# Hybrid diffusion backbone on one core: sums of squares read from the SBUF copies, values split first

## The chip, the core and the metric

The kernel runs on one core of a Trainium2 chip. A core has a matrix engine (TensorE; PE in the profile, with its weight loads as PEld), a vector engine (VectorE; DVE), an activation engine (ScalarE; ACT), GpSimd (POOL) and SyncE (SP), which issues DMA here. Each engine runs its own queue in order, and engines wait for each other by semaphores. Matrix products land in banks of PSUM; everything else lives in SBUF. The metric is the device time of one execution in microseconds, lower is better.

## What is computed

Two layers over 256 latent tokens and 256 context tokens, 512 rows of width 1024 in four row tiles `tt` of 128. In each layer a normed input goes through one wide projection into three mixers (a bidirectional Mamba-2 scan, windowed attention, multi-head latent attention) and gates; the mixers are projected back, gated and summed, and a SwiGLU network follows. What matters here is that keys, queries and latents are RMS-normed, each over its own last axis:

```
def rms_norm(x, g):
    y = xf * lax.rsqrt(jnp.mean(xf * xf, axis=-1, keepdims=True) + EPS)
    return (y * g.astype(F32)).astype(x.dtype)

def kv_heads(k, v):                       # windowed attention
    return rms_norm(k.reshape(shp), k_g), v.reshape(shp)

kv = (rms_norm(ckv, kv_lat_g) @ w_ukv).reshape(bsz, n, MLA_HEADS, MLA_NOPE + MLA_V)
k_nope = rms_norm(kv[..., :MLA_NOPE], k_g[:MLA_NOPE])      # latent attention; the rest of kv are values
q = (rms_norm(cq, q_lat_g) @ w_uq).reshape(bsz, n, MLA_HEADS, MLA_QK)
```

So each of these norms needs a sum of squares of a product that lies in PSUM, and the product itself in SBUF. Values are not normed.

## The kernel before

**Products in three parts.** Every fp32 product is made of three matmuls (`mm3`, L147 to L149): both factors are split into a high part `hi` and a rest `lo`, and hi·hi, hi·lo and lo·hi are summed in a PSUM bank. `hilo` (L150) splits a PSUM result so: ACT writes the high part (L154), then DVE subtracts it from the same bank (L155; with a scale L157 and L158). `wsplit` (L124) does the same with weights that a DMA brought: ACT at L133, DVE at L135, into three buffers (NHI), with a priority of 200 over other work. Attention's probabilities are split by `hilo` too (`pth`, `ptl`).

**Banks.** `PS` hands out PSUM tiles of one bank: four tagged `mm`, two `s`, two `t`. A product that needs a bank waits until the last reader of the result in it is done.

**The stages that the change touches.** `ssm_inproj` copies the latents `lat` and the rope keys `kro` (L725, L726) and squares both (L727, L728). `swa_kv` makes the keys and values of windowed attention: four banks, one for each row tile, 256 key columns and 256 value columns each. For each tile ACT copies the keys (`kraw`, L1063), squares both heads with a running sum into `ssk` (L1066, twice), and `hilo` splits the values into `vh` and `vl`. Behind the four tiles DVE scales `ssk` (L1070), POOL raises it to the power -1/2 (`rsk`, L161), and the keys are multiplied by it (L1076: on DVE in layer 0, on POOL in layer 1). DVE then rotates the first two tiles (`ro`, `rt`, L606 to L614), and PE transposes them (L1089). `swa_q` copies and squares the queries (L1104, L1106). `mla_prep` does so with the query latents (L1208, L1210). `mla_pair` runs four times in each layer, for two heads at a time: one bank for each tile again, with two squares (L1247), the key copy (L1248) and the split of the values, and then for the queries a square (L1266) and a copy (`qraw`, on DVE for even tiles of layer 0, else on ACT).

**What sets the order.** The stages are generators. `weave` and `braid` run them between the products of the gates (`gates`, L1354), the scan of the Mamba branch (`z`, `xs`, `ef`, `eb`, `cb`, `yo` and `hst` in the rows) and attention. A scheduling framework then lays the instructions into one fixed queue for each engine, from the order of the code, its priorities and its own estimates of durations, and puts in the semaphore waits. It keeps two engines from reading the same PSUM bank at the same time: in the queues below, a reader of a bank waits for the reader ahead of it on the other engine.

## Time and profile before

| | us |
|---|---|
| median of 3 runs (lowest, highest) | 1848.68 (1847.68, 1849.12) |
| the profiled execution | 1848.97 |
| its span in the trace | 1847.2 |
| PE busy in it | 1801.7 (98%) |
| DVE busy | 1406.7 (76%) |
| ACT busy | 920.5 (50%) |
| POOL busy | 268.2 (15%) |

The span is what the trace covers; the 1.8 us beside it lie around the program. The mean granted clock of PE was 0.997 of full speed. In a timeline row the number in brackets is how long that engine stood idle before the row, and what ended the wait; a row with no bracket began as soon as its engine was free or waited too briefly to be listed. In a row of waits the three numbers are us in total, times, and the longest one.

### The profile page before, as it was taken

Reading aid. Unit: us, or ns where it says so; the run is one execution under the profiler, and the core shown is the slowest. Engines: PE = TensorE matmul, PEld = TensorE weight load, DVE = VectorE, ACT = ScalarE, POOL = GpSimd, SP = SyncE. Lnnn points to the kernel's source line nnn. Section 1 sums busy time; section 2 is a strip of 40 time slices with the busy share of each in tenths; the row PEclk is TensorE's granted clock in tenths of the full one; section 3 lists DMA queues with packets and bytes.
Section 4 is the critical chain, followed back from the end, with each engine's and each line's share of the span. In section 5 each row is a group of like instructions: output and inputs, shape, how many; then the busy total and the mean of one; then the engine's idle time right before and its main releaser. Section 6 shows DMA issues by size and latency. Waiting matters only on the chain.

```text
span 1847.2 us, 28430 instructions
## 1 busy us (share of the span) xinstructions
PE 1801.7 (98%) x10198; PEld 1541.2 (83%) x10198; DVE 1406.7 (76%) x3094; ACT 920.5 (50%) x2026; POOL 268.2 (15%) x242
## 2 busy tenths in 40 slices
PE   8999999999999999999999999999999999999999
PEld 3886777788878888898888888886779988899999
DVE  3896876798798885569888875797788688786654
ACT  2557674455555653342323222547756767455442
POOL 1004432100013331100000000002420022210000
PEclk9999999999999999999999999999999999999999
DMA  8334352454443333535556553335334332255564
GB/s 303 92 105 148 116 175 97 153 187 154 151 152 105 99 120 119 185 115 198 188 186 201 184 189 117 104 104 182 109 132 147 107 95 88 90 180 171 183 181 139
DMA packets 101405, 270.22 MB, mean 146 GB/s; under 512 B 11504, under 2 KB 14320, under 8 KB 101264
## 3 DMA queue, kind: packets, MB, share of 16 engines
q1 hardware_dynamic: 94032, 254.37, 42.5%
q10 hardware_dynamic: 5904, 9.71, 1.5%
q0 software_dynamic: 1328, 4.33, 0.6%
q8 instruction: 80, 1.31, 0.3%
q14 instruction: 61, 0.50, 0.1%
HBM read 256.70 MB, written 11.67 MB: 145 GB/s over the span
## 4 chain that ended last, share of the span: by engine, by line
PE 70%; DVE 6%; ACT 3%; issue 3%; POOL 1%; DMA 1%; SPq 0%; POOLq 0%; DVEq 0%; ACTq 0%
PE mm L147 21%; PE mm L148 21%; PE mm L149 21%; DVE lo L135 2%; PE t L647 1%; ACT hi L133 1%; PE s L147 1%; PE s L149 1%; PE s L148 1%; DVE ptl L155 0%; DVE cv L814 0%; PE t L1317 0%; DMA eb<-scr 0%; DVE eb L962 0%; POOL xd L903 0%
## 5 line engine op out<-in xcount | busy, mean ns | idle before, releaser
L133 ACT ACTIVATE hi<-raw 128x1024 fp32r<-128x1024 f32 (+1 forms) x350 | 356.6, 1021 | 575.6 <-PE mm L148 316.4
L135 DVE TENSOR_TENSOR lo<-raw,hi 128x1024 fp32r<-128x1024 f32 (+1 forms) x350 | 426.0, 1220 | 194.7 <-ACT hi L133 192.8
L147 PE MATMUL mm<-hh,hi 128*128 128x512 f32 (+1 forms) x1280 | 438.6, 345 | 2.2 <-DVE vl L155 1.5
L149 PE MATMUL mm<-hh,lo 128*128 128x512 f32 (+1 forms) x1280 | 436.0, 341 | 0.9 <-DVE lo L135 0.9
L148 PE MATMUL mm<-hl,hi 128*128 128x512 f32 (+1 forms) x1280 | 436.1, 342 | 0.7 <-DVE hl L400 0.7
L147 PEld LDWEIGHTS mm<-hh,hi 128*128 128x128 f32 x1280 | 241.7, 190 | 30.0 <-DVE vl L155 2.0
L149 PEld LDWEIGHTS mm<-hh,lo 128*128 128x128 f32 x1280 | 242.5, 190 | 28.6 <-DVE lo L135 1.3
L148 PEld LDWEIGHTS mm<-hl,hi 128*128 128x128 f32 x1280 | 242.6, 190 | 28.4 <-DVE hl L400 1.3
L147 PE MATMUL mm<-hi,hh 128*128 128x512 f32 (+2 forms) x368 | 142.6, 388 | 3.5 <-DVE z L871 1.4
L149 PE MATMUL mm<-hi,hl 128*128 128x512 f32 (+2 forms) x368 | 137.8, 382 | 1.8 <-DVE hl L400 1.8
L148 PE MATMUL mm<-lo,hh 128*128 128x512 f32 (+2 forms) x368 | 139.5, 379 | 0.0
L271 DVE CUSTOM_DVE_ANT_0 junk<-mraw,crow,mod 128x512 bf16<-128x512 f32 x160 | 120.2, 751 | 5.2 <-DMA mraw<-in_w_modT 2.9
L271 DVE CUSTOM_DVE_ANT_0 junk<-mraw,crow 128x512 bf16<-128x512 f32 x160 | 110.2, 689 | 12.0 <-DMA mraw<-in_w_modT 10.7
L154 ACT ACTIVATE pth<-t 128x256 fp32r<-128x256 f32 x160 | 60.3, 388 | 50.8 <-DVE ptl L155 42.2
L147 PEld LDWEIGHTS mm<-hi,hh 128*128 128x128 f32 x368 | 70.0, 190 | 17.9 <-DVE z L871 2.5
L149 PEld LDWEIGHTS mm<-hi,hl 128*128 128x128 f32 x368 | 69.7, 191 | 14.0 <-DVE hl L400 2.1
L148 PEld LDWEIGHTS mm<-lo,hh 128*128 128x128 f32 x368 | 70.0, 190 | 11.9 <-issue 2.9
L147 PE MATMUL mm<-acth,hi 128*128 128x512 f32 (+1 forms) x198 | 72.7, 367 | 0.6 <-DVE xl L1416 0.6
L149 PE MATMUL mm<-acth,lo 128*128 128x512 f32 (+1 forms) x198 | 72.4, 365 | 0.0
L148 PE MATMUL mm<-actl,hi 128*128 128x512 f32 (+1 forms) x198 | 72.4, 365 | 0.0
L814 DVE SCALAR_TENSOR_TENSOR cv<-cx,c_kb,cv 128x508 f32<-128x508 f32 (+3 forms) x96 | 70.6, 736 | 1.8 <-ACT cv L805 0.4
L155 DVE TENSOR_TENSOR ptl<-t,pth 128x256 fp32r<-128x256 f32 x160 | 65.4, 415 | 7.8 <-ACT pth L154 7.4
(422 smaller groups left out, 3973.1 us busy)
## 6 DMA issues: line engine op xcount, KB each, us to landing
raw<-in_w_fi SPq DMA_DIRECT2D x88, 512.0 KB, 3.4
mraw<-in_w_modT SPq DMA_DIRECT2D x160, 256.0 KB, 4.5
raw<-in_w_g SPq DMA_DIRECT2D x48, 512.0 KB, 3.3
raw<-in_w_p SPq DMA_DIRECT2D x48, 512.0 KB, 3.3
raw<-in_w_fo SPq DMA_DIRECT2D x32, 512.0 KB, 3.9
raw<-in_w_xbc SPq DMA_DIRECT2D x24, 512.0 KB, 3.5
wm<-in_w_mod SPq DMA_DIRECT2D x32, 256.0 KB, 5.4
raw<-in_w_z SPq DMA_DIRECT2D x16, 512.0 KB, 3.3
```

The costliest lines, as they stand in the source:

```text
L133: nc.scalar.activation(hi[:, :n], raw[:, :n], AF.Copy)
L135: eng.tensor_tensor(lo[:, :n], raw[:, :n], hi[:, :n].bitcast(F32), ALU.subtract)
L147: mm(out, a[0], b[0], start=start, stop=False)
L148: mm(out, a[0], b[1], start=False, stop=False)
L149: mm(out, a[1], b[0], start=False, stop=stop)
L154: nc.scalar.activation(hi, src, AF.Copy)
L155: nc.vector.tensor_tensor(lo, src, hi.bitcast(F32), ALU.subtract)
L271: nc.vector.tensor_tensor_reduce(junk, raw[j], self.crow[2 * s + j], 0.5, o if j else 0.0, ALU.mult, ALU.add, o)
L647: nc.tensor.transpose(tp[:, i * P : (i + 1) * P], pt[:, i * P : (i + 1) * P], self.ident)
L814: nc.vector.scalar_tensor_tensor(r3(v)[:, :, o], r3(x)[:, :, i], w[:, m, j : j + 1], r3(v)[:, :, o], ALU.mult, ALU.add)
```

## The change

All sums of squares of these stages read the copy in SBUF and no longer the bank. In `swa_kv` the split of the values stands ahead of the key copy of each tile, and the squares of all four tiles stand in a second loop. In `swa_q` the squares of all tiles stand behind the copies. In `mla_pair` each tile has the split first, then the key copy, then the squares; the query copy stands ahead of its square. By count 138 squares change their source: L727 8, L728 8, L1066 16, L1106 12, L1210 6, L1247 64, L1266 24. No instruction is added or taken away. Lines of the new kernel stand 1 to 4 further down (L1063 becomes L1064, L1066 L1069, L1070 L1072, L1076 L1078, L1089 L1091, L1247 L1252, L1248 L1249).

```
@@ -724,8 +724,8 @@ ssm_inproj
             self.copy(l and tt % 2 == 0, lat[tt], ps[:, 0:256])
             nc.scalar.activation(kro[:, tt, :], ps[:, 256:320], AF.Copy)
-            nc.scalar.activation(sq[:, 0:256], ps[:, 0:256], AF.Square, accum_out=ssl[:, tt : tt + 1])
-            nc.scalar.activation(sq[:, 256:320], ps[:, 256:320], AF.Square, accum_out=ssl[:, 4 + tt : 5 + tt])
+            nc.scalar.activation(sq[:, 0:256], lat[tt], AF.Square, accum_out=ssl[:, tt : tt + 1])
+            nc.scalar.activation(sq[:, 256:320], kro[:, tt, :], AF.Square, accum_out=ssl[:, 4 + tt : 5 + tt])
@@ -1060,11 +1060,13 @@ swa_kv
         for tt in range(4):
             o = slice((tt % 2) * 256, (tt % 2) * 256 + 256)
+            self.hilo(vh[tt // 2][:, o], vl[tt // 2][:, o], pss[tt][:, 256:512])
             nc.scalar.activation(kr[tt // 2][:, o], pss[tt][:, 0:256], AF.Copy)
+        for tt in range(4):
             sq = self.U(name="sq")
             for j in range(2):
-                nc.scalar.activation(sq[:, 0:P], pss[tt][:, j * P : (j + 1) * P], AF.Square, accum_out=ss[:, tt, j : j + 1])
-            self.hilo(vh[tt // 2][:, o], vl[tt // 2][:, o], pss[tt][:, 256:512])
+                o = (tt % 2) * 256 + j * P
+                nc.scalar.activation(sq[:, 0:P], kr[tt // 2][:, o : o + P], AF.Square, accum_out=ss[:, tt, j : j + 1])
@@ -1103,7 +1105,8 @@ swa_q
             nc.scalar.activation(qr[tt], pss[tt], AF.Copy)
             sq[tt] = self.U(name="sq")
-            nc.scalar.activation(sq[tt], pss[tt], AF.Square)
+        for tt in tts:
+            nc.scalar.activation(sq[tt], qr[tt], AF.Square)
@@ -1207,7 +1210,7 @@ mla_prep
-            nc.scalar.activation(sq[:, 0:384], pss[tt][:, 0:384], AF.Square, accum_out=ss[:, tt : tt + 1])
+            nc.scalar.activation(sq[:, 0:384], cq[tt][:, 0:384], AF.Square, accum_out=ss[:, tt : tt + 1])
@@ -1242,11 +1245,11 @@ mla_pair, keys and values
+            self.hilo(o3(vh[tt // 2]), o3(vl[tt // 2]), pv[:, :, 1, :])
+            nc.scalar.activation(o3(kr[tt // 2]), pv[:, :, 0, :], AF.Copy)
             sq = self.U(name="sq")
             for j in range(2):
-                nc.scalar.activation(sq[:, 0:P], pv[:, j, 0, :], AF.Square, accum_out=ss[:, tt, j : j + 1])
-            nc.scalar.activation(o3(kr[tt // 2]), pv[:, :, 0, :], AF.Copy)
-            self.hilo(o3(vh[tt // 2]), o3(vl[tt // 2]), pv[:, :, 1, :])
+                nc.scalar.activation(sq[:, 0:P], kr[tt // 2][:, o][:, j * P : (j + 1) * P], AF.Square, accum_out=ss[:, tt, j : j + 1])
@@ -1263,8 +1266,8 @@ mla_pair, queries
-            nc.scalar.activation(sq[:, 0:384], ps[:, 0:384], AF.Square)
             self.copy(l == 0 and tt % 2 == 0, qr[tt][:, 0:384], ps[:, 0:384])
+            nc.scalar.activation(sq[:, 0:384], qr[tt][:, 0:384], AF.Square)
```

In the queues below a row is one instruction: its line, its operation, what it writes and reads, and the engines that it waits for (`Activation` is ACT, `Pool` POOL, `DMAHW...` a transfer). A row without brackets waits for nothing that its engine has not waited for already.

In ACT's queue at the window keys of layer 1, this stood before. `mm_12782` to `mm_12785` are the banks of the four row tiles, `hi_13159` a weight of the third gate product from there, `hi_13203` of the fourth:

```order
L1063 ACTIVATE kraw_13003<-mm_12782 128x256 [waits PE_49]
L1066 ACTIVATE sq_13007,ssk_13005<-mm_12782 128x128
L1066 ACTIVATE sq_13007,ssk_13005<-mm_12782 128x128 [waits Activation_49]
L154 ACTIVATE vh_12999<-mm_12782 128x256
L1063 ACTIVATE kraw_13003<-mm_12783 128x256 [waits PE_49]
```

Each tile has these four rows; `hi_13159` stands behind the third tile and `hi_13203` behind the fourth. In the same place ACT has now:

```order
L154 ACTIVATE vh_12999<-mm_12782 128x256 [waits PE_49]
L1064 ACTIVATE kraw_13003<-mm_12782 128x256 [waits DVE_49]
L154 ACTIVATE vh_12999<-mm_12783 128x256 [waits PE_49]
L1064 ACTIVATE kraw_13003<-mm_12783 128x256 [waits DVE_49]
L154 ACTIVATE vh_13000<-mm_12784 128x256 [waits PE_49]
L1064 ACTIVATE kraw_13004<-mm_12784 128x256 [waits DVE_49]
L1069 ACTIVATE sq_13018,ssk_13005<-kraw_13003 128x128 [waits Activation_49]
L133 ACTIVATE hi_13159<-raw_13157 128x1024 [waits DMAHW4_49,PE_49]
L154 ACTIVATE vh_13000<-mm_12785 128x256
...
L133 ACTIVATE hi_13203<-raw_13201 128x1024 [waits DMAHW1_49,PE_49]
L1064 ACTIVATE kraw_13004<-mm_12785 128x256 [waits DVE_49]
```

Every key copy has come behind the split's DVE half and waits for DVE; in the gap stand five squares, and two squares follow the last row, with a gate copy between them. On DVE, in the same stretch, stood before:

```order
L998 TENSOR_TENSOR z_12664<-z_12664,xs_12434 128x512 [waits Pool_49]
L155 TENSOR_TENSOR vl_13001<-mm_12782,vh_12999 128x256 [waits PE_49,Activation_49]
L155 TENSOR_TENSOR vl_13001<-mm_12783,vh_12999 128x256 [waits PE_49,Activation_49]
L155 TENSOR_TENSOR vl_13002<-mm_12784,vh_13000 128x256 [waits PE_49,Activation_49]
L135 TENSOR_TENSOR lo_13160<-raw_13157,hi_13159 128x1024 [waits DMAHW4_49,Activation_49]
L1070 TENSOR_SCALAR ssk_13005<-ssk_13005 128x8 [waits Activation_49]
```

And now:

```order
L155 TENSOR_TENSOR vl_13001<-mm_12782,vh_12999 128x256 [waits Activation_49]
L998 TENSOR_TENSOR z_12664<-z_12664,xs_12434 128x512 [waits Pool_49]
L155 TENSOR_TENSOR vl_13001<-mm_12783,vh_12999 128x256 [waits Activation_49]
L155 TENSOR_TENSOR vl_13002<-mm_12784,vh_13000 128x256 [waits Activation_49]
L135 TENSOR_TENSOR lo_13160<-raw_13157,hi_13159 128x1024 [waits DMAHW4_49,Activation_49]
L155 TENSOR_TENSOR vl_13002<-mm_12785,vh_13000 128x256 [waits PE_49,Activation_49]
L135 TENSOR_TENSOR lo_13204<-raw_13201,hi_13203 128x1024 [waits DMAHW1_49,PE_49,Activation_49]
L1072 TENSOR_SCALAR ssk_13005<-ssk_13005 128x8 [waits Activation_49]
```

The first `vl` went ahead of `z`, which waits for POOL, and the scaling of `ssk` went behind the fourth `vl` and `lo_13204`. In layer 0 ACT's queue at the window keys reads now:

```order
L154 ACTIVATE vh_1937<-mm_1692 128x256 [waits PE_49]
L154 ACTIVATE vh_1937<-mm_1693 128x256 [waits PE_49]
L1064 ACTIVATE kraw_1941<-mm_1692 128x256 [waits DVE_49]
L1064 ACTIVATE kraw_1941<-mm_1693 128x256 [waits DVE_49]
L154 ACTIVATE vh_1938<-mm_1694 128x256 [waits PE_49]
L1064 ACTIVATE kraw_1942<-mm_1694 128x256 [waits DVE_49]
L1069 ACTIVATE sq_1956,ssk_1943<-kraw_1941 128x128 [waits Activation_49]
L133 ACTIVATE hi_2130<-raw_2128 128x1024 [waits DMAHW2_49,PE_49]
...
L1064 ACTIVATE kraw_1942<-mm_1695 128x256 [waits DVE_49]
```

Before, it had the four rows of each tile in the order shown for layer 1, and the second to fourth `vl` stood on DVE behind a `z` that waits for POOL, as they do now. The scaling of `ssk` stood ahead of the fourth `vl` and stands behind it now. In the gap are the fourth split and five squares.

## Rows read from the trace of the kernel before

**Rows 1.** Page, part 1: busy us (share of the span) xinstructions.

```profile
PE 1801.7 (98%) x10198; PEld 1541.2 (83%) x10198; DVE 1406.7 (76%) x3094; ACT 920.5 (50%) x2026; POOL 268.2 (15%) x242
```

**Rows 2.** Waits of PE, whole span: us in total, times, longest us.

```profile
PE mm L147 <- ACT pth L154: 5.0, 10, 0.9
...
PE mm L147 <- DVE vl L155: 1.5, 1, 1.5
...
PE t L982 <- DVE kTl L158: 1.4, 1, 1.4
```

**Rows 3.** Groups of ACT by line and shape: count | busy us, mean ns.

```profile
L947 ACT ACTIVATE eb<-eb,du 128x128 f32<-128x128 f32 x96 | 36.4, 389 | 1.5 <-DMA eb<-scr 1.5
...
L1066 ACT ACTIVATE sq<-mm 128x128 f32<-128x128 f32 x16 | 4.4, 276 | 0.3
```

**Rows 4.** DVE timeline: start us, us, line, operation [idle before <-releaser]; latent queries.

```profile
500.43 0.56 DVE L141 COPY qraw<-mm 128x384 f32<-128x384 f32 x1 [0.95 <-ACT sq L1266]
```

**Rows 5.** DVE timeline, window keys of layer 1.

```profile
1307.33 0.69 DVE L998 TENSOR_TENSOR z<-z,xs 128x512 f32<-128x512 f32 x1 [3.99 <-POOL xs L992]
...
1307.94 1.08 DVE L155 TENSOR_TENSOR vl<-mm,vh 128x256 fp32r<-128x256 f32 x3
...
1310.07 0.16 DVE L1070 TENSOR_SCALAR ssk<-ssk 128x8 f32<-128x8 f32 x1
...
1314.82 0.51 DVE L606 TENSOR_TENSOR ro<-kraw,rs 128x256 f32<-128x256 f32 x1
...
1318.12 0.41 DVE L614 TENSOR_TENSOR ro<-ro,rt 128x256 f32<-128x256 f32 x1
```

**Rows 6.** ACT timeline, same stretch.

```profile
1303.27 0.37 ACT L1063 ACTIVATE kraw<-mm 128x256 f32<-128x256 f32 x1
...
1303.53 0.27 ACT L1066 ACTIVATE sq<-mm 128x128 f32<-128x128 f32 x1
...
1304.19 0.38 ACT L154 ACTIVATE vh<-mm 128x256 fp32r<-128x256 f32 x1
...
1306.91 1.06 ACT L133 ACTIVATE hi<-raw 128x1024 fp32r<-128x1024 f32 x1
```

**Rows 7.** POOL timeline, same stretch.

```profile
1310.31 1.65 POOL L161 TENSOR_TENSOR rsk<-ssk,mhalf 128x8 f32<-128x8 f32 x1 [3.01 <-DVE ssk L1070]
...
1312.03 3.02 POOL L1076 TENSOR_TENSOR kraw<-kraw,rsk 128x512 f32<-128x512 f32 x2
```

**Rows 8.** PE timeline, same stretch: first gate product, first key transposes.

```profile
1308.41 0.39 PE L147 MATMUL mm<-hh,hi 128*128 128x256 f32 x1 [1.53 <-DVE vl L155]
...
1319.97 0.38 PE L1089 MATMUL t<-c_ka,ro 128*128 128x128 f32 x2
```

**Rows 9.** DVE timeline, window keys of layer 0.

```profile
221.71 0.69 DVE L998 TENSOR_TENSOR z<-z,xs 128x512 f32<-128x512 f32 x1 [0.94 <-POOL xs L992]
...
225.22 0.16 DVE L1070 TENSOR_SCALAR ssk<-ssk 128x8 f32<-128x8 f32 x1
...
227.17 1.29 DVE L1076 TENSOR_TENSOR kraw<-kraw,rsk 128x512 f32<-128x512 f32 x2 [1.45 <-POOL rsk L161]
...
229.29 1.22 DVE L135 TENSOR_TENSOR lo<-raw,hi 128x1024 fp32r<-128x1024 f32 x1 [0.83 <-ACT hi L133]
...
235.90 1.23 DVE L135 TENSOR_TENSOR lo<-raw,hi 128x1024 fp32r<-128x1024 f32 x1 [1.07 <-ACT hi L133]
...
243.89 0.41 DVE L614 TENSOR_TENSOR ro<-ro,rt 128x256 f32<-128x256 f32 x1
```

**Rows 10.** PE timeline, second key transpose of layer 0.

```profile
244.36 0.33 PE L1089 MATMUL t<-c_ka,ro 128*128 128x128 f32 x1 [0.90 <-DVE ro L614]
```

**Rows 11.** Waits of PE in 540:620, 630:720 and 1530:1610 (latent pairs).

```profile
PE mm L147 <- ACT pth L154: 0.9, 1, 0.9
...
PE mm L147 <- ACT pth L154: 1.7, 4, 0.8
...
PE mm L147 <- ACT pth L154: 1.2, 2, 0.6
```

## The prediction

> **What bounds the kernel now.** I read the page first: PE is busy 98% of the span, DVE 76%, ACT 50% [rows 1]. So ACT has time to spare on average, and work given to it or taken from it moves the end only where PE stands and waits. The next view is therefore the table of PE's waits. For the banks that this change wants to empty sooner it holds a single entry, "PE mm L147 <- DVE vl L155", 1.5 us, once [rows 2]; that entry is the ceiling of what a bank handed over earlier can give directly. The largest entry is a wait for `pth`, an ACT instruction of attention, 5.0 us in ten pieces [rows 2]. Then I read timelines of ACT, DVE and POOL around the two window-key stages, since there DVE, POOL and PE depend on the last square, and last the queues of the new kernel against those of the old.
>
> **What one square costs.** The count does not change, the source does. An ACT instruction of 128x128 takes 276 ns from PSUM (L1066) and 389 ns from SBUF (L947, another function) [rows 3]. These are durations that overlap their neighbours: a 0.37 us copy at 1303.27 is followed by a square at 1303.53 in the same queue [rows 6]. So 113 ns is the upper bound for one square; zero is the lower bound; I take half, 0.05 us, since about a tenth of a us of each duration lies under the next one. For 138 squares that is 7 us (bounds 0 and 15.6) on an engine that idles half the span. I cost it at nothing except in the two chains below, where eight squares lie in a row: 0.4 us each.
>
> The Trainium skill ("Perfetto Trace Analysis", section "Optimizing Scalar/DVE Operations") speaks against this change: it gives ScalarE a fixed access overhead of about 93 ns on SBUF and about 51 ns on PSUM, so a read from the copy is the dearer one. By it a square would cost 42 ns more, an estimate of 5.8 us over 138 and 0.3 us in each chain; the rows above point the same way.
>
> **What the order costs.** The framework does not let two engines read a bank together. The trace of before shows the rule from the other side: a DVE copy of queries stands 0.95 us idle at 500.43 until ACT's square has left the bank [rows 4]. Eight such copies get free of the square, and that wait sits on DVE where PE does not wait, so I count nothing for it. The price is that each `kraw` copy, formerly ahead of the split, now waits for DVE's `vl` of its bank: 8 in `swa_kv`, 32 in `mla_pair`. Whatever DVE is stuck on, ACT is then stuck on too, and behind it in ACT's queue stand the squares, the weights' `hi` and the gates' copies.
>
> **Layer 1, window keys.** Bank 0 is full at 1303.27, when ACT's first copy starts [rows 6]. Now `vh` (0.38) and the first `vl` (0.42; it stands ahead of `z` now) and `kraw` (0.37) empty it by about 1304.5, where before `vl` came at 1307.94 behind a `z` that waited 3.99 us for POOL [rows 5]. PE's first gate product then needs no wait and starts at 1308.41 - 1.53 = 1306.88 [rows 8]. Gain: **1.5 us**.
>
> Then the second `kraw` waits for the second `vl`, which is still behind `z`: `vl` at 1307.94 to 1308.36. ACT stands from 1304.8 to 1308.4 with nothing else to do. From there, in the new order: `kraw` 0.3, `vh` 0.3, `vl` 0.4, `kraw` 0.3, one square 0.5 (it needs the copy's end, and a read of the sum) make 1310.2; the weight `hi` takes 1.06 [rows 6], `vh` 0.3, five squares at 0.38 make 1313.4; the next `hi` 1.06, `kraw`, a square, a gate's copy and the last square together 1.5 make 1315.9. Before, `ssk` was scaled at 1310.07 [rows 5]. Now it is scaled at about 1316.0, 5.9 us later. POOL's `rsk` (1.65) and the first half of its key product (1.51 of 3.02) follow [rows 7] and end at 1319.4. Before, that half ended at 1313.5 and the rotation began at 1314.82, because DVE had other work in between [rows 5]; now DVE waits for it. The rotation is thus 4.6 us late, and ends, one `eb` shorter between, some 4.3 us behind its old end of 1318.53 [rows 5], at 1322.8. PE reaches the transposes at 1319.97 - 1.53 = 1318.44 [rows 8] and stands 4.4 us. Net of the gain: +2.9. The 1.4 us that PE waits for `kTl` soon after [rows 2] shrink by some 0.4, as PE comes later by 2.9 and `kTl` by about 2.5. **+2.5 us** in all. Bounds: -1.5, if ACT does not stand behind `z` and the rotation stays inside its old slack of 1.4 us; +4.0, if all of the lateness arrives and nothing shrinks.
>
> **Layer 0, window keys.** Here the first `vl` came ahead of `z` before too, and PE had no bank wait to lose. The second `kraw` waits for the `vl` behind `z` (221.71, waiting for POOL) [rows 9], so ACT goes on at about 222.8. The same list of steps then ends with `ssk` at about 229.3 where it was at 225.22: 4.1 us late. The keys' product with `rsk` on DVE moves with it, from 227.17 to 231.3. Behind it DVE had 0.83 us of idle at 229.29 and 1.07 us at 235.90 [rows 9], both for a weight's `hi` that need not move; these take up 1.9. The last `ro` at 243.89 [rows 9] comes 2.2 us later, and PE, which already waited 0.90 for it [rows 10], waits about 3. **+2.0 us**, bounds 0 (all taken up) and +3.
>
> **Latent pairs and the rest.** In `swa_q`, `mla_prep` and `ssm_inproj` no wait of PE hangs on a bank or a square: 0, bounds ±1. In the eight pairs ACT loses two squares ahead of each split and gets a wait for DVE; where PE waits there, it is for `pth` in seven cases, 0.9 + 1.7 + 1.2 = 3.8 us [rows 11]. I take 0, with bounds -3.8 (all of these go) and +4 (half a us more for each pair, about one `vl`).
>
> **The sum.** 1848.97 (the profiled execution, 0.29 above the median) + 2.5 + 2.0 = 1853.5; against the median of 1848.68 that is 1853.2. I say **1853 us**.
>
> **The rivals.** *Not slower: the banks win.* Place: the eight pairs, and the gate product at 1308.41. Before, 0.66 us of squares (1303.53 to 1304.19 in the window keys, alike in the pairs) stood ahead of the split of every bank [rows 6]. If a `kraw` waits for its `vl` for less than that 0.66, each bank is free sooner, `pth` queued behind gets its turn sooner, and PE gains up to 3.8 + 1.5: 1848.7 - 5.3 = 1843.4, with half of it 1846. Against it speaks the 3.99 us of DVE at `z`, six times that point; for it, that most `vl` of the pairs have no such `z` ahead.
>
> *Nothing arrives.* The late squares are there, but DVE's and PE's slack takes them up, or the two terms and the gain of 1.5 cancel: 1848 to 1851. For it speaks that PE waited at neither rotation by more than 0.9 before; against it, that the lateness is three times the slack.
>
> *The pairs pay too.* ACT parked behind DVE holds `pth` and `prob` back in the pairs, where both engines are fuller than elsewhere: at half a us to a whole one for each of the eight, 4 to 8 more, 1857 to 1861.
>
> *The change doesn't do what it says.* A bank is not emptied earlier at all where `kraw` waits for `vl` and `vl` is late; that is the forecast's own mechanism, and needs no chance of its own.
>
> **How the numbers follow.** Forecast (1851.5 to 1855.5) 0.42; the banks win (1843.4 to 1848) 0.22; nothing arrives 0.22; the pairs pay 0.14. The measurement can tell about 0.2%, 3.7 us, from no change, so slower begins at 1852.4 and faster below 1845.0. Three quarters of the forecast and all of the pairs' rival are slower: 0.31 + 0.14 = 0.45. About half of the banks' rival is faster: 0.12. The rest is 0.43. The range of 8 in 10 leaves out the lower part of the banks' rival (0.13) and the upper part of the pairs' (0.07): 1846 to 1858. The forecast's own range is 1851.5 to 1855.5.
>
> **What would show it.** Right: no wait of PE at the first gate product of layer 1; an ACT idle of about 3.6 us before the second `kraw`, ended by DVE `vl`; `ssk` near 1316; PE waiting some 4 us for `ro` at the transposes of layer 1 and 3 at those of layer 0. Wrong: `ssk` before 1311 there, or PE waits for `ro` under 1 us; then the lateness was taken up, or the steps between the waits are shorter than I made them. A sum of waits for `pth` that moved by over 2 us would hand the result to the pairs.

## The result: 0.83% slower, more than three times what was forecast

The changed kernel takes 1863.79 us (median of 4 runs, 1862.49 to 1865.13) against 1848.18 us (4 runs of the kernel before beside them), a ratio of 1.0083 with a 95% interval of 1.0071 to 1.0095. The sign was right, the size was not: +15.6 us measured, +4.5 forecast, and the time lies above the stated range.

| us | before | after |
|---|---|---|
| median | 1848.18 | 1863.79 |
| span of the profiled execution | 1847.2 | 1862.2 |
| PE busy | 1801.7 | 1808.2 |
| PE idle (span less busy) | 45.5 | 54.0 |

PE issues the same 10198 matmuls. Of 15.0 us more span 8.5 are waits, and 6.5 are matmuls that took longer. Part 1 of the page of the changed kernel (busy us, share of the span, instructions), to be read beside [rows 1]:

```profile
PE 1808.2 (97%) x10198; PEld 1544.0 (83%) x10198; DVE 1409.9 (76%) x3094; ACT 925.9 (50%) x2026; POOL 265.9 (14%) x242
```


The waits of PE in the changed kernel (what waited, for whom; then us in total, times, the longest), beside [rows 2]:

```profile
PE t L1091 <- DVE ro L614: 6.6, 4, 3.2
PE t L647 <- DVE ptl L155: 5.1, 5, 2.4
PE mm L147 <- ACT pth L154: 4.7, 10, 0.8
PE t L1287 <- DVE kTl L158: 2.1, 1, 2.1
```


The wait of 1.5 us for `vl` at the first gate product is gone from the table, as the change means it. The waits for `ro` rose from 0.9 to 6.6 us, and those of the probabilities' transposes for `ptl` from 1.3 to 5.1 us. The wait for `pth`, with which two of the rivals worked, did not move (5.0 and 4.7).

### The profile page after: what moved, and what is told of

It is laid out like the page before. It is cut to its first block, busy times and chain, and to the rows that moved or that the text cites. A ratio compares the mean times of both kernels' runs of the same rounds, so it can differ in the third digit from the quotient of the medians.

```text
span 1862.2 us, 28415 instructions
## 1 busy us (share of the span) xinstructions
PE 1808.2 (97%) x10198; PEld 1544.0 (83%) x10198; DVE 1409.9 (76%) x3094; ACT 925.9 (50%) x2026; POOL 265.9 (14%) x242
## 4 chain that ended last, share of the span: by engine, by line
PE 68%; DVE 6%; issue 3%; ACT 3%; POOL 2%; DMA 2%; SPq 0%; POOLq 0%; ACTq 0%; DVEq 0%
PE mm L147 21%; PE mm L148 20%; PE mm L149 20%; DVE lo L135 2%; PE t L647 1%; ACT hi L133 1%; DMA mraw<-in_w_modT 1%; PE s L147 1%; PE s L149 1%; PE s L148 1%; DVE ptl L155 0%; POOL gate L1396 0%; DVE junk L271 0%; DVE cv L814 0%; PE t L1320 0%
## 5 line engine op out<-in xcount | busy, mean ns | idle before, releaser
L148 PEld LDWEIGHTS mm<-lo,hh 128*128 128x128 f32 x368 | 69.7, 189 | 11.9 <-issue 2.9
```

Source lines behind the costliest of these rows:

```text
L148: mm(out, a[0], b[1], start=False, stop=False)
```

## Where the time went

PE's matmuls can be paired by their number in the two traces, since there are as many in both. The difference of their start times, taken at a few places, tells in which stretch the changed kernel falls back. This is worked out from the traces' start times (in each place the median over 25 matmuls); stretches are in time of the kernel before, and the experiments of the next section stand beside. PE's own order is not the same everywhere: between 575 and 607 us it differs from the kernel before in all kernels but e6 and e10, so a bound in there sets different matmuls side by side. The rows 563-583 and 583-613 therefore count only together. Three rows set apart by "of which" or "together" have their bounds where the orders agree.

| stretch, what runs there | after | e1 | e2 | e3 | e4 | e5 | e6 | e8 | e9 | e10 | e11 | e12 |
|---|---|---|---|---|---|---|---|---|---|---|---|---|
| 242-252, window keys, layer 0 | 3.6 | 0.0 | 3.7 | 0.0 | 0.0 | 0.0 | 0.0 | 2.3 | 0.0 | 0.0 | 0.0 | 0.0 |
| 388-423, window attention, layer 0 | 2.8 | 2.0 | 2.0 | 2.8 | 1.9 | 0.0 | 1.8 | 0.0 | 0.0 | 0.0 | 0.0 | 0.0 |
| 548-563, latent pairs, layer 0 | 1.2 | 0.8 | 0.3 | 0.0 | 0.0 | 0.3 | 0.0 | 0.0 | 0.0 | 0.0 | 0.0 | 0.2 |
| 563-583, the same | 4.5 | 4.1 | 2.4 | 3.8 | 2.7 | 2.5 | 0.0 | 4.9 | 3.3 | 0.0 | 1.8 | 1.0 |
| 583-613, the same | -1.7 | -1.7 | -1.7 | -1.7 | -1.7 | -1.7 | 0.0 | -1.7 | -1.7 | 0.0 | -1.5 | -1.2 |
| 548-613, the three together | 4.0 | 3.2 | 1.0 | 2.1 | 1.0 | 1.0 | 0.0 | 3.2 | 1.6 | 0.0 | 0.3 | 0.0 |
| 613-701, the same | 2.5 | 2.6 | 2.5 | 1.2 | 1.3 | 1.3 | 0.1 | 1.6 | 0.7 | 0.0 | 0.1 | 2.1 |
| of which 671-701 | 1.4 | 1.5 | 1.3 | 0.0 | 0.1 | 0.0 | 0.0 | 1.4 | 0.1 | 0.0 | 0.1 | 1.0 |
| 1283-1331, window keys, layer 1 | 3.0 | 0.0 | 3.0 | 1.0 | 0.2 | 0.0 | 0.0 | 3.0 | 0.0 | -0.1 | 0.0 | 0.0 |
| 1486-1598, latent pairs, layer 1 | 0.0 | 1.5 | -1.5 | -0.5 | 2.1 | -0.1 | -0.2 | 0.8 | -0.1 | -1.5 | 0.0 | -0.1 |
| of which 1530-1598 | 1.1 | 1.1 | -0.1 | 1.3 | 2.3 | 0.0 | 0.0 | 2.5 | 0.0 | 0.0 | 0.0 | -0.1 |
| whole trace | 15.0 | 10.1 | 10.1 | 6.9 | 7.3 | 3.9 | 1.8 | 11.8 | 2.1 | -3.9 | -0.4 | 3.1 |

What is missing to the last row lies in small pieces and in the first 242 us; the differences there, -2.2 (e10) to +1.9 (e5), arise before 200 us, ahead of any edit of these two, and so differ from execution to execution. So the window keys cost 6.6 us, the latent pairs of layer 0 6.6, and the window attention of layer 0 2.8. The 0.0 of the pairs of layer 1 hides 1.1: in the trace of the kernel before PE ran at 0.50 of full clock in 1518 to 1521, and in that of the changed kernel it did not, which gives 1.0 back. Every trace is one execution, and a stretch at half clock that comes in one and not in another is worth 1 to 1.5 us in such a table (last section).

**Window keys of layer 1.** Three timelines of the changed kernel follow (start, duration, engine, line, operation, and in brackets the idle time ahead of it with what ended that); to compare with [rows 5 to 7], subtract 11.9 us, by which the trace is late at 1283. First ACT:

```profile
1316.02 0.39 ACT L1064 ACTIVATE kraw<-mm 128x256 f32<-128x256 f32 x1 [0.49 <-DVE vl L155]
...
1321.13 0.38 ACT L1064 ACTIVATE kraw<-mm 128x256 f32<-128x256 f32 x1 [4.45 <-DVE vl L155]
...
1322.28 0.38 ACT L1064 ACTIVATE kraw<-mm 128x256 f32<-128x256 f32 x1 [0.49 <-DVE vl L155]
...
1327.44 0.30 ACT L1069 ACTIVATE sq<-kraw 128x128 f32<-128x128 f32 x1
```


DVE in the same stretch:

```profile
1315.57 0.42 DVE L155 TENSOR_TENSOR vl<-mm,vh 128x256 fp32r<-128x256 f32 x1 [0.32 <-ACT vh L154]
1319.24 1.52 DVE L998 TENSOR_TENSOR z<-z,xs 128x512 f32<-128x512 f32 x1 [3.26 <-POOL xs L992]
1320.68 0.41 DVE L155 TENSOR_TENSOR vl<-mm,vh 128x256 fp32r<-128x256 f32 x1
...
1327.87 0.17 DVE L1072 TENSOR_SCALAR ssk<-ssk 128x8 f32<-128x8 f32 x1
...
1330.91 1.24 DVE L606 TENSOR_TENSOR ro<-kraw,rs 128x256 f32<-128x256 f32 x1 [1.86 <-POOL kraw L1078]
...
1334.10 0.41 DVE L614 TENSOR_TENSOR ro<-ro,rt 128x256 f32<-128x256 f32 x1
```


POOL in the same stretch:

```profile
1316.56 2.66 POOL L992 TENSOR_TENSOR xs<-xs,yo 128x512 f32<-128x512 f32 x2
1319.17 1.04 POOL L903 TENSOR_TENSOR xd<-xs,du 128x512 f32<-128x512 f32 x1
1328.12 1.65 POOL L161 TENSOR_TENSOR rsk<-ssk,mhalf 128x8 f32<-128x8 f32 x1 [7.90 <-DVE ssk L1072]
1329.84 2.04 POOL L1078 TENSOR_TENSOR kraw<-kraw,rsk 128x512 f32<-128x512 f32 x2
```


The first `vl` (1315.57) stands ahead of `z` now and the first copy follows it. Then the second copy waits 4.45 us for a `vl` that stands behind `z`, which itself waits for POOL and takes 1.52 us, beside POOL's `xd`, where it took 0.69. The last square runs at 1327.44 and `ssk` is scaled at 1327.87, that is 1316.0 in the old count, to the tenth what the working gave; that is luck, since the wait ended 0.8 us later than forecast (1309.2 in the old count for 1308.4) and the steps behind it took 6.6 us and not 7.5. The rotation ends at 1334.5, or 1322.6 in the old count (forecast 1322.8).

The page "PSUM — Partial Sum Buffer" of the Trainium skill (section "PSUM bank collisions raise a hardware error") says that software has to keep reads of one bank by two engines apart, reads of ScalarE and VectorE too. The trace shows the framework doing so, for other columns of the bank too: the copy starts only when `vl` has ended, 4.45 us later than ACT was free. What unguarded reads would do no run here shows.

The timeline of PE in the changed kernel, behind that:

```profile
1333.43 0.47 PE L1091 MATMUL t<-c_ka,ro 128*128 128x128 f32 x1 [3.18 <-DVE ro L614]
1334.56 0.47 PE L1091 MATMUL t<-c_ka,ro 128*128 128x128 f32 x1 [0.67 <-DVE ro L614]
```


The windows of the same stretch (from and to, their length, then busy us and count of PE, PEld, DVE, ACT and POOL, the granted clock, the DMA share, GB/s):

```profile
1329.00:1332.00 3.00, 1.24 (x11) 1.04 (x9) 1.14 (x2) 3.00 (x9) 2.80 (x3) 1.00 0.75 240
1332.00:1335.00 3.00, 0.91 (x3) 0.62 (x4) 3.00 (x16) 2.89 (x8) 0.00 (x0) 0.54 0.00 1
1335.00:1338.00 3.00, 3.00 (x16) 3.00 (x15) 3.00 (x5) 1.01 (x4) 1.37 (x1) 0.50 0.23 70
1338.00:1341.00 3.00, 3.00 (x22) 2.89 (x21) 3.00 (x8) 1.22 (x3) 0.11 (x1) 0.82 0.90 262
```


PE waits 3.18 and 0.67 us, 3.85 together (forecast 4.4). The windows show what the working did not hold: behind the wait the clock stands at 0.50, the lower of the two levels, 1.2 GHz, until past 1338, and the same 256-column matmuls start 0.21 us apart where they started 0.12 apart. That adds 2.0 us. The wait for `kTl` that followed in the kernel before is hidden by it and gives its 1.4 [rows 2] back.

**Window keys of layer 0.** The same, with 0.55 and 2.17 us of waiting where there were 0.90 [rows 10]. PE's timeline in the changed kernel:

```profile
243.30 0.30 PE L1091 MATMUL t<-c_ka,ro 128*128 128x128 f32 x1 [0.55 <-DVE ro L614]
245.76 0.33 PE L1091 MATMUL t<-c_ka,ro 128*128 128x128 f32 x1 [2.17 <-DVE ro L614]
```


Its windows, with half clock behind the second wait:

```profile
244.00:247.00 3.00, 1.24 (x7) 1.09 (x8) 3.00 (x8) 1.07 (x2) 0.42 (x1) 0.97 0.23 87
247.00:250.00 3.00, 3.00 (x9) 2.32 (x8) 2.73 (x10) 2.92 (x10) 0.00 (x0) 0.50 0.68 235
250.00:253.00 3.00, 3.00 (x15) 2.43 (x14) 1.86 (x5) 1.03 (x4) 0.00 (x0) 0.96 0.61 115
```


Of the 3.6 us here 1.8 are waits (0.55 + 2.17 - 0.90); the other 1.8 lie where the clock is down.

**Latent pairs of layer 0.** Between 575 and 590 us of the changed kernel PE waits for a `prob` and then for a `ptl`, and runs at 0.68 of full clock in the 5 us behind. Its timeline in the changed kernel:

```profile
580.79 0.50 PE L147 MATMUL s<-kTh,qTh 128*128 128x512 f32 x1 [1.54 <-ACT prob L683]
...
584.60 0.97 PE L647 MATMUL t<-c_ka,prob 128*128 128x128 f32 x4 [2.39 <-DVE ptl L155]
```


The windows of that stretch:

```profile
580.00:585.00 5.00, 1.82 (x8) 1.30 (x9) 5.00 (x16) 3.43 (x11) 1.99 (x1) 0.97 0.15 41
585.00:590.00 5.00, 5.00 (x18) 4.08 (x17) 4.44 (x11) 4.34 (x10) 4.92 (x5) 0.68 0.60 210
```


In the kernel before PE waited 1.57 us at that place and the clock held at 1.00 (572 to 579). PE's timeline in the kernel before:

```profile
574.33 0.63 PE L647 MATMUL t<-c_ka,prob 128*128 128x128 f32 x4 [1.57 <-DVE nm L678]
```

The row names `nm`, but the wait is for the `ptl` just ahead of it on DVE: there as in e5, e11 and e12 these transposes start 0.14 to 0.15 us after that `ptl` ends.

Of the 4.0 us at 548 to 613, 2.3 lie at 560 to 571, where besides the changed kernel only e1 (1.5) and e8 (0.6) lose more than 0.3, the other kernels with the split first in the pairs. Of the 2.5 behind 613, 0.6 are a longer wait for `kTl` and 1.4 the half clock behind that wait. PE's timeline and window there in the changed kernel:

```profile
682.24 0.66 PE L1287 MATMUL t<-c_ka,kraw 128*128 128x128 f32 x4 [2.05 <-DVE kTl L158]
...
684.00:687.00 3.00, 3.00 (x13) 2.70 (x13) 2.82 (x12) 1.20 (x4) 0.71 (x2) 0.50 0.84 287
```

In the kernel before this wait was 1.46 us. In e7, which is the changed kernel with an addition elsewhere, it is 2.05 us again and the clock holds:

```profile
679.38 0.66 PE L1290 MATMUL t<-c_ka,kraw 128*128 128x128 f32 x4 [2.05 <-DVE kTl L158]
...
681.00:684.00 3.00, 3.00 (x21) 2.62 (x22) 3.00 (x14) 1.85 (x6) 0.57 (x2) 1.00 0.86 288
```

**The price of a square.** In the groups of ACT the squares of the window keys are 303 ns long from SBUF where they were 276 [rows 3]. Rows overlap, so what a square costs ACT is read from one start to the next: in a row of five, 293 ns from SBUF (changed kernel) and 250 ns from the bank (e8, below), 43 more. Over 138 squares that would be an estimated 5.9 us. ACT is busy 925.9 us where it was 920.5, but its copies and accumulator reads changed too, so the 5.4 us are not the squares' alone. Two groups of ACT in the changed kernel (count, busy us and mean ns, then the idle time ahead and what ended it):

```profile
L1069 ACT ACTIVATE sq<-kraw 128x128 f32<-128x128 f32 x16 | 4.8, 303 | 0.1
...
L1270 ACT ACTIVATE sq<-qraw 128x384 f32<-128x384 f32 x24 | 12.6, 526 | 6.6 <-DVE qraw L141 5.3 <-DMA raw<-in_w_ukv 1.1
```


The Trainium skill, page "Perfetto Trace Analysis", section "Optimizing Scalar/DVE Operations", has an access of ScalarE to SBUF 42 ns dearer than one to PSUM (93 and 51), which would be an estimated 5.8 us for 138. The trace agrees from start to start (43 ns); the lengths of the rows differ by 27. Two neighbouring squares of the changed kernel, then of e8:

```profile
1324.06 0.31 ACT L1069 ACTIVATE sq<-kraw 128x128 f32<-128x128 f32 x1
...
1324.35 0.30 ACT L1069 ACTIVATE sq<-kraw 128x128 f32<-128x128 f32 x1
...
1319.44 0.29 ACT L1068 ACTIVATE sq<-mm 128x128 f32<-128x128 f32 x1
...
1319.69 0.30 ACT L1068 ACTIVATE sq<-mm 128x128 f32<-128x128 f32 x1
```

The row of `qraw` among the groups shows the other cost of the order: 5.3 us in which ACT stood for DVE's copy of queries.

## The experiments

Three theories stood against each other. A: ACT waits for DVE's half of the split, squares and all that is behind them come late, PE stalls and pays with its clock. B: the squares are dearer from SBUF. C: the framework's queues came out in another order elsewhere, and that costs. All times below are medians; the kernel before ran beside each (1848.7 to 1849.2 us).

**e1, the window keys put back.** `swa_kv` as before, all else as changed.

> The changed kernel with the window keys' part alone put back (`swa_kv` as it was: copy, squares from the bank, split). Theory A (the key copy that waits for DVE's half of the split makes ACT stand, the squares come late, PE stalls at the key transposes and runs on at half clock): the two window-key places give back what they cost between the two traces, 3.6 us in layer 0 and 3.3 in layer 1, so about 1857. Theory B (the squares are dearer from SBUF): only 16 of 138 squares change back, under 2 us, so about 1862 to 1863. Theory C (the framework's queues came out worse elsewhere, and these two places do not matter): 1863.

1858.66 us, ratio 1.0049 (1.0030 to 1.0067). Both window-key stretches fall to 0.0 in the table: what they cost comes from this part alone. The rest of the loss stays.

**e2, the latent pairs' keys and values put back.**

> The changed kernel with the keys-and-values part of the latent pairs alone put back (squares from the bank, copy, split; 64 squares). Theory A: of the 8.7 us that the new trace is longer between 340 and 675 us, the 6 that arise in the pairs of layer 0 (from 530 us on) go, so about 1857 to 1858, with the two window-key stalls still there. Theory B: 64 of 138 squares, about half of the loss, 1856. Theory C: any value between 1848 and 1866, with losses at other places than the pairs.

1859.54 us, ratio 1.0054 (1.0039 to 1.0069). The window keys lose as in the changed kernel (3.7 and 3.0). But the pairs of layer 0 still lose 3.5, 1.0 at 548 to 613 and 2.5 behind, so their loss has a second source, outside of the part put back.

**e3, copy ahead of the split.** In `swa_kv` and, likewise, in `mla_pair`:

```
-            self.hilo(vh[tt // 2][:, o], vl[tt // 2][:, o], pss[tt][:, 256:512])
             nc.scalar.activation(kr[tt // 2][:, o], pss[tt][:, 0:256], AF.Copy)
+            self.hilo(vh[tt // 2][:, o], vl[tt // 2][:, o], pss[tt][:, 256:512])
```

> The changed kernel with one pair of lines swapped in `swa_kv` and in `mla_pair`: the key copy stands ahead of the split again, the squares stay behind both and read SBUF. No key copy waits for DVE then. Theory A: the loss goes, 1847 to 1850, with no stall of 2 us and more at the key transposes and no half clock behind them; where the first bank of layer 1 is handed on early, the 1.5 us wait at the first gate product shrinks. Theory B: the squares still read SBUF, so 1862 to 1864.

1855.89 us, ratio 1.0034 (1.0023 to 1.0045), against 1.0083 for the changed kernel. Swapping two lines takes back over half of the loss; theory B, which saw nothing change, falls. Theory A expected all of it back, and that falls too: the window attention still loses 2.8, the pairs 3.3, and 1.0 is left at the window keys of layer 1, where PE now waits 2.25 us for `kTl` and runs at 0.56 of full clock behind (1332 to 1335). In layer 1 ACT no longer waits for DVE; its timeline in e3:

```profile
1309.51 0.37 ACT L1063 ACTIVATE kraw<-mm 128x256 f32<-128x256 f32 x1
...
1316.90 0.29 ACT L1069 ACTIVATE sq<-kraw 128x128 f32<-128x128 f32 x1
```


**e4, the source alone.** The order of before, squares from SBUF.

> The order of the kernel before in `swa_kv` and `mla_pair` (copy, squares, split in each tile; in the pairs the copy goes ahead of its squares), with every square reading its SBUF copy. Theory A: no copy waits for DVE, so 1847 to 1850. Theory B: all 138 squares read SBUF, so 1862 to 1864; if only ACT's extra time of some 7 us arrives, 1855.

1855.19 us, ratio 1.0028 (1.0019 to 1.0038). The window keys lose 0.0 and 0.2. The loss lies at 388 to 423 (1.9), in the pairs of layer 0 (2.3, as in e5, which changes the queries alone) and in the pairs of layer 1 (2.3 at 1530 to 1598), with queues that came out in another order there; the number is the one that theory B named for "ACT's extra time arrives", but ACT's extra time is spread over all squares, and this loss is not. Whether the dearer squares or the new order make it at these places this run can't tell.

**e5, the queries of the pairs alone** (square behind the copy, from the copy).

> The kernel before with one part of the change alone: in `mla_pair` the query copy stands ahead of its square and the square reads the copy (24 squares; for 8 of them, layer 0, the copy is on DVE, so ACT's square now waits for DVE). Theory A, widened by the four runs so far (ACT waits for DVE here too, and the framework's queues around it come out in another order): the piece that all four runs lost between 571 and 580 us, 2.6 to 3.8, arises here too, with a wait of PE at the probabilities' transposes (`t` by `ptl`) of over 2 us, then -1.4 near 600 and +1.2 near 670: 1849 + 2.4 = about 1851.5. Theory B (dearer source): 24 of 138 squares, 1850. Rival: nothing arrives here, 1849, and the piece belongs to the other stages.

1851.21 us, ratio 1.0012 (1.0003 to 1.0021). The piece at 563 to 583 is there, 2.5, and so are the -1.7 and +1.3 that follow; together the pairs of layer 0 lose 2.3. PE waits there as in the changed kernel; its timeline in e5:

```profile
578.04 0.63 PE L647 MATMUL t<-c_ka,prob 128*128 128x128 f32 x4 [2.74 <-DVE ptl L155]
```


**e6, latents, window queries and query latents alone.**

> The kernel before with the change in `ssm_inproj`, `swa_q` and `mla_prep` alone (34 squares from SBUF, no copy moved behind anything on DVE but two squares in layer 1). The four runs so far all lose 1.9 to 2.8 us between 385 and 423 us, where the query latents and the window attention of layer 0 run. Theory A: that piece belongs here and nothing else does, 1849 + 2 = 1851. Theory B: 34 of 138 squares, 1850.5, spread. Rival: nothing, 1849.

1850.95 us, ratio 1.0010 (1.0001 to 1.0020). The piece at 388 to 423 belongs here, 1.8. No square in it waits for DVE in layer 0; on DVE a weight's split went ahead of a `ptl` just in front of it too, at 378 to 381, and whether that is the cause was not tried.

**e8, the order alone.** `swa_kv` and the pairs' keys and values: split, copy, squares, all from the bank.

> The kernel before with the order of the change in `swa_kv` and the keys-and-values part of `mla_pair` alone: split first, then the key copy, then the squares, which still read the PSUM bank. No square reads SBUF. Theory A: the copy waits for DVE as in the changed kernel, the squares come as late; the window keys lose some 7 us again, the pairs 2 to 3: 1856 to 1859. Theory B (the source is what costs): 1848 to 1850.

1859.47 us, ratio 1.0047 (1.0029 to 1.0066). With no square on SBUF the window keys lose 2.3 and 3.0 again (3.6 and 3.0 in the changed kernel), and the pairs of layer 0 4.8. In layer 1 ACT waits for DVE as in the changed kernel; its timeline in e8:

```profile
1316.55 0.38 ACT L1064 ACTIVATE kraw<-mm 128x256 f32<-128x256 f32 x1 [3.61 <-DVE vl L155]
```


At the window keys the order does it, not the source (e4: 0.0 and 0.2). In layer 1 part of the 3.0 comes by another road than in the changed kernel: the late squares still hold the banks, and PE's first gate product waits 2.25 us for one of them. e5, e6 and e8 are three parts of the change; their traces are 3.9, 1.8 and 11.8 us longer, the whole one 15.0.

**e7, filling the wait.** The changed kernel, with matmuls that nobody reads where PE stands:

```
             ps = self.PS("t")
+            if g == 0:
+                for _ in range((9, 14)[l]):
+                    nc.tensor.matmul(ps, h[0][0][:, 0:P], h[0][0][:, 0:512], start=True, stop=True)
```

> The changed kernel with 9 (layer 0) and 14 (layer 1) matmuls of 128x512 added on PE right ahead of the first key transposes of the windowed attention, about 2.0 and 3.2 us of work that nobody reads, in the time in which PE stands there anyway. Theory A says that each of these stalls also cost a stretch at half clock (granted clock 0.50), some 1.6 and 2.0 us: with PE busy through most of the wait the clock stays at 1.0 and the time falls by 2 to 3.6 us, 1860 to 1862, though work was added. Rival (the clock has nothing to do with the wait): the added work fills idle time and changes nothing, or adds up to 1 us: 1863.5 to 1865.

1862.12 us, ratio 1.0076 (1.0061 to 1.0091): 1.7 us under the changed kernel, at the edge of the forecast, and the two intervals overlap, so the time alone settles nothing. The trace says more. In layer 0 the added work ends at 243.6, the last `ro` still comes late, and the clock stays up. PE's timeline in e7:

```profile
241.31 2.33 PE L1091 MATMUL t<-hh 128*128 128x512 f32 x9
...
244.61 0.33 PE L1094 MATMUL t<-c_ka,ro 128*128 128x128 f32 x1 [0.86 <-DVE ro L614]
```


The windows of e7 behind it:

```profile
244.00:247.00 3.00, 2.39 (x12) 2.04 (x13) 2.73 (x8) 1.07 (x4) 0.00 (x0) 1.00 0.35 102
247.00:250.00 3.00, 3.00 (x15) 2.48 (x14) 3.00 (x10) 3.00 (x11) 0.00 (x0) 1.00 0.97 284
```


In 247 to 250 PE issues 15 matmuls at clock 1.00, where the changed kernel issued 9 at 0.50. The stretch loses 2.05 us and no longer 3.6. In layer 1 the clock stays at 1.00 as well and 2.0 us are won by 1335, but then PE waits 2.37 us for `kTl`: what the clock gave went into the next wait, and the stretch ends 0.85 us later than in the changed kernel. Another 1.4 us by which this trace is shorter lie near 680, where nothing was added and the clock held by itself. So the time shows a gain in layer 0 at most, 1.6 us.

**e9, only the queries whose copy is on ACT.** Tiles with a copy on DVE keep their square from the bank ahead of it.

> The kernel before with the query part of `mla_pair` changed only where the copy is on ACT (16 of 24 squares: odd tiles of layer 0, all of layer 1). The 8 tiles whose copy is on DVE keep their square from the bank ahead of the copy, so no ACT square waits for DVE. Theory A (the loss of the queries' part alone, 2.5 us, comes from ACT's square waiting for DVE's copy): the piece between 571 and 580 us goes, 1848 to 1849.5, no stall of over 2 us at the probabilities' transposes there. Rival (the source, or any new order, is enough): 1851 again.

1850.28 us, ratio 1.0007 (0.9997 to 1.0016), not to be told from no change, but the trace answers: 548 to 613 loses 1.6 (3.3 and -1.7), and PE waits as in the changed kernel. Its timeline in e9:

```profile
575.53 1.09 PE L647 MATMUL t<-c_ka,prob 128*128 128x128 f32 x4 [2.84 <-DVE ptl L155]
```


No square of the queries waits for DVE in layer 0 of this kernel. Theory A falls for this place. What the eight kernels that lose most there share (the changed one, e1 to e5, e8, e9) is the order on DVE: in the kernel before, and in e6 and e10, `ptl_5928` stands ahead of `lo_6216`, a weight's split of 1.2 us, and in the eight it stands behind. DVE's rows there, in short:

```
before:  ptl_5926, ..., ptl_5928, nm_5935, lo_6216
after:   ptl_5926, ..., nm_5935, lo_6216, ptl_5928
```

`ptl_5928` is the last reader of the bank that PE's next four transposes need.

**e11, that swap as the only edit**, in the kernel before: the weight's DVE half gets 100 more priority, no square is touched. The framework then changes the queues behind it too, up to 607 us.

> The kernel before, with no square touched: one weight's split on DVE (`lo_6216`, keys and values of the third latent pair of layer 0) has its priority raised by 100, which puts it ahead of the probabilities' `ptl_5928` in DVE's queue, as it stands in all eight kernels that lose 2.5 to 4.4 us between 571 and 580 us (the changed kernel among them), and as it does not stand in the three that lose nothing there. Theory C for this place (the new order in DVE's queue is the cause, whatever squares read): a wait of PE for `ptl` of over 2 us arises there, half clock behind it, 1851 to 1852. Rival (the order is a companion, and the squares' waits or source are the cause): 1848.5 to 1849.5.

1848.91 us, ratio 1.0000 (0.9991 to 1.0009). The wait came as expected, the time did not: PE waits 2.55 us there where it waited 1.57, and the clock falls to 0.55, but over 548 to 613 the kernel loses 0.3 us, where the changed kernel loses 4.0. PE's timeline in e11:

```profile
574.63 0.63 PE L648 MATMUL t<-c_ka,prob 128*128 128x128 f32 x4 [2.55 <-DVE nm L679]
```


The window of e11 behind that wait:

```profile
576.00:579.00 3.00, 3.00 (x9) 2.31 (x8) 3.00 (x6) 2.10 (x5) 2.03 (x3) 0.55 0.71 264
```


**e12, the swap undone** in the kernel of e5.

> The kernel with the query part of `mla_pair` alone changed (24 squares read the copy), and the same weight's split on DVE lowered by 100 in priority, so that it stands behind `ptl_5928` again. Theory C for this place: the loss of 2.5 us between 571 and 580 us goes, 1848.5 to 1849.5. Rival (ACT's square that waits for DVE's copy, or the source): 1851 stays.

1851.86 us, ratio 1.0016 (1.0007 to 1.0025), no better than e5. At 548 to 613 the loss of 1.0 goes, PE waits 2.23 us and the clock holds; then 613 to 701 loses 2.1 where e5 lost 1.3, because the clock falls behind a wait for `kTl` of 2.06 us that e5 had too, at full clock. PE's timeline in e12:

```profile
576.58 0.63 PE L648 MATMUL t<-c_ka,prob 128*128 128x128 f32 x4 [2.23 <-DVE nm L679]
```

So the order on DVE moves the wait at that place, in both directions, but it is worth 0.3 us in one kernel and 1.0 in the other, less than the timed runs can tell, and putting one pair of rows right does not put the kernel right.

**e10, copy, split, squares by tile** in `swa_kv` alone, the rest as before:

```
             nc.scalar.activation(kr[tt // 2][:, o], pss[tt][:, 0:256], AF.Copy)
+            self.hilo(vh[tt // 2][:, o], vl[tt // 2][:, o], pss[tt][:, 256:512])
             sq = self.U(name="sq")
             for j in range(2):
-                nc.scalar.activation(sq[:, 0:P], pss[tt][:, j * P : (j + 1) * P], AF.Square, accum_out=ss[:, tt, j : j + 1])
-            self.hilo(vh[tt // 2][:, o], vl[tt // 2][:, o], pss[tt][:, 256:512])
+                q = (tt % 2) * 256 + j * P
+                nc.scalar.activation(sq[:, 0:P], kr[tt // 2][:, q : q + P], AF.Square, accum_out=ss[:, tt, j : j + 1])
```

> The kernel before with one change in `swa_kv` alone: each tile has the key copy, then the split, then its two squares from the SBUF copy. The copy waits for PE only, the squares for ACT only, and the first DVE half of layer 1 stands ahead of the `z` that waits for POOL. Theory A: the wait of 1.5 us at the first gate product of layer 1 goes, nothing comes late, so 1847 to 1848, 1.0 to 1.6 us under the kernel before. Rival (squares from SBUF, or what the framework makes of the new order, cost more than that): 1849 to 1851.

1848.10 us, ratio 0.9998 (0.9989 to 1.0006): no change. The 1.5 us wait at the first gate product is gone and nothing is late, and yet the stretch gains 0.1, because PE now arrives sooner at the next wait. Its timeline in e10, and the window behind the wait:

```profile
1324.20 1.10 PE L982 MATMUL t<-hst,cv 128*128 128x512 f32 x2 [3.02 <-DVE kTl L158]
...
1324.00:1327.00 3.00, 2.79 (x11) 1.66 (x12) 2.54 (x5) 3.00 (x11) 0.00 (x0) 1.00 0.59 179
```


That wait for `kTl` was 1.4 us [rows 2] and is 3.0, and the clock holds at 1.00 behind it. So even the one bank wait that this change could remove was worth nothing: DVE sets the time there, not the bank. (The profiled execution of e10 is 3.9 us shorter than that of before, but only 0.1 of it lies in this stretch; 1.5 lie in the pairs of layer 1, where the clock did not fall this time, and the rest in the first 242 us. The timed runs show none of it.)

## The prediction, step by step

- **What bounds the kernel, and the ceiling of the gain**: right. One wait for such a bank, 1.5 us, and it went. That the 1.5 us come back at `kTl` (e10) was not foreseen.
- **What a square costs**: right within its bounds: 43 ns from start to start for the window keys, where 50 were put down. At the window keys none of it is visible by itself: with all squares on SBUF in the old order they lose 0.0 and 0.2 (e4), with none on SBUF in the new order 2.3 and 3.0 (e8).
- **The key copy waits for DVE**: right. Putting the copies ahead takes back more than half of the loss (e3: 1.0083 to 1.0034): 5.6 us at the window keys and 2.3 at 560 to 571 in the pairs; e8 shows it without the source. Another 1.4 us of what e3 gives back is the fall of the clock near 680, which can't be put to the copies, since the wait ahead of it is in e3 too.
- **Layer 1, window keys** (+2.5 forecast, +3.0 measured): `ssk` and the rotation came within 0.4 us of the forecast, but ACT's wait was 4.45 us (3.6 forecast), the steps behind it shorter, and PE's wait 3.85 (4.4 forecast). The sum came near by errors that cancel: 2.0 us of half clock were missing, and against them stand 0.55 us less wait and 1.4 us that came back at `kTl` where 0.4 was put down.
- **Layer 0, window keys** (+2.0 forecast, +3.6 measured): the waits came out near the forecast, 1.8 us more than before (though `ssk` was 3.2 us late and not 4.1), and the **half clock** behind them was left out, 1.8 us by the trace, of which filling the wait took back 1.6 (e7: 3.6 to 2.05). This is a term of the sum that was missing: a wait was priced as its own length.
- **Latent pairs and the rest** (0 forecast, with bounds of -3.8 and +4, and 0 within 1 for window queries and latents): **this is the step that failed**. Measured were +6.6 for the pairs of layer 0 and +2.8 for the window attention, 9.4 of the 15 us. It asked whether a wait of PE hangs on a bank or a square today. It asked it of the queue order of the kernel before. The edit put ACT's copies behind DVE there as at the window keys (2.3 us at 560 to 571), and it gave DVE, ACT and PE a new order in stages that it does not touch: at 574 PE already waited 1.57 us for DVE, at full clock, and with a weight's split of 1.2 us in front of a `ptl` it waits 2.4 to 2.8, with half clock behind. That swap is one part among several: alone it costs 0.3 us (e11).
- **The rivals**: "the pairs pay too" (0.14) came nearest; its 1857 to 1861 lack the 3.8 us of half clock at the window keys. Its mechanism was half right: copies parked behind DVE do cost in the pairs (e3 loses 3.3 us there where the changed kernel loses 6.6, of which 2.3 at 560 to 571), but the queries' part costs 2.3 without them (e5), and no run parts its squares' source from the new order. "The banks win" was wrong: the waits for `pth` did not move.

What stays open: what makes the 2 to 3 us at 388 to 423, which of the many rows that changed places make the wait for `kTl` near 680 longer by 0.6 us, and what decides whether the clock falls behind a given wait. e11 and e12 settle one pair of rows at one place, not these.

## What to carry to other kernels

Before an instruction is moved ahead of a reader of the same PSUM bank on another engine, look at what that engine is stuck on at the time: the wait is inherited, and so is everything queued behind. Price a new wait of the matrix engine as its length, with a stretch at half clock behind it as the upper bound (1.0 to 2.0 us here), and look at the waits that are there already: at 574 us here a wait of 1.57 us had full clock behind it, and one of 2.39 or more had half clock in every trace. Compare a stretch in several traces before putting a microsecond of half clock down to an edit. Where a framework lays out the queues, a change in one stage must be read in the queues of all stages that run beside it, above all where an engine is nearly full.

## What the runs showed of the hardware

PE's granted clock went down to its lower level, 1.2 GHz, behind waits of PE that had been priced as their own length. In the changed kernel it stood at 0.50 behind the waits of 3.18 and 0.67 us in layer 1, and again behind the 2.17 us in layer 0; in e11 at 0.55 behind 2.55 us. In e7, with 0.86 and 0.81 us of wait left at the two places, it held at 1.00. At 0.50 PE got through 9 matmuls of the same stream in 3 us, at 1.00 through 15 (247 to 250 of the changed kernel and of e7). Such a fall cost 1.0 us (e12, near 680) to 2.0 us (layer 1) beside the wait itself.

The length of a wait does not decide it alone. At the latent pairs of layer 0 the clock held behind 1.57 us (kernel before, and 1.58 in e6 and e10) and 2.23 (e12), and fell in all nine traces with 2.39 to 2.84. But near 680 it fell behind a wait of 2.05 us in the changed kernel, e1, e2 and e12 and held behind the same wait in e3, e4, e5, e7 and e9; in e10 it held behind 3.02 us; and in the kernel before it fell to 0.50 at 1518 to 1521, behind waits of 1.08 and 0.75 us, where in e10, with the same order on PE and the same two waits, it held (1.00 in 1515 to 1518) and the stretch is 1.5 us shorter. What else decides it no run shows.

A `z` of 128x512 on DVE took 1.52 us while POOL ran its `xd`, and 0.69 where it did not (changed kernel and before, layer 1); another, beside POOL's `ef`, took 0.69 too (kernel before, at 278).
